# Four buffers for each half of a split weight, the up products' pieces 32 bytes lower, room taken from the dynamic DMAs' scratch

## The chip, the core and the metric

The kernel runs on one core of a Trainium2 chip. The core has a matrix engine (TensorE, PE in the profile, with its weight loads as PEld), a vector engine (DVE), a scalar engine (ACT), GpSimd (POOL) and a queue engine that issues DMAs (SP). All of them work on SBUF, a memory of 128 partitions; an address below is a byte address within a partition. The metric is the device time of one execution in microseconds. Before the change it is 1057.3 us, the median of three runs (1056.95 to 1057.44).

## What is computed

Two decoder layers on 512 tokens of width 1024, in float32: a latent attention mixer and a gated linear attention mixer, each followed by a squared-ReLU MLP with 4096 hidden columns. The part that matters here is the MLP:

```python
def sq_relu_mlp(xn, w_up, w_down):
    hid = jnp.square(jax.nn.relu(xn @ w_up))
    return hid @ w_down

for i in range(DEPTH):              # DEPTH = 2
    xn = rms_norm(x, norm_mix[i])
    x = x + mixer_i(xn)
    x = x + sq_relu_mlp(rms_norm(x, norm_mlp[i]), mlp_w_up[i], mlp_w_down[i])
return rms_norm(x, final_norm)
```

## The kernel before

**Split products.** Every large product is made of three matrix products in float32r: each operand is split into a rounded part (hi) and a rest (lo), and hi x hi, hi x lo and lo x hi are added in PSUM. For weights this is `piece` (L137): it takes a part of a raw weight tile, at most 1,024 float32 per partition, ACT writes the hi part into a tile with the tag `wh` (L104) and DVE the lo part into one with the tag `wl` (L107). Each tag has three buffers of 4,096 bytes, used in turn by all stages, so a fourth piece can be split only when the matmuls of the first have read it.

**The MLP.** `mlp` handles 512 hidden columns at a time, eight blocks in all. The first block and the last have code of their own (`up_first`, and the code behind the loop); the seven between are steps of a Strassen-like scheme (`step`) with seven up products and seven down products in place of eight and eight. An up product (`up_product`, L931, its matmuls in L939) takes four k-tiles of 128, two column halves and three parts: 24 matmuls whose stationary operand is a 128x128 block of the piece (`wh` or `wl`) and whose moving operand is 256 columns of the input. A down product (`down_product`, L941, matmuls in L948) has 12 matmuls whose moving operand is 512 columns of the piece and whose stationary operand is a block of the hidden values. The step's up products come in the order "11", "21", "T2", "T1", "22", "T3", "T4", a down product behind each. For "11", "21" and "22" the moving operand lies in the tiles with the tag `set` that the norm wrote (hi and lo 2,048 bytes apart); for the four with T it lies in tiles `T1` to `T4`, which `quadrants` (L864) fills with sums of input quarters (hi and lo 1,024 bytes apart). A step runs seven times in each of the two MLPs.

**Transfers.** Raw weights come by DMAs that SP issues. Where two weight quarters are added on the way, the second comes by an accumulating DMA that POOL issues (L918, L928): four of them per step. POOL's DMAs keep their descriptors in a scratch at the bottom of SBUF, 16,384 bytes per partition unless the program says otherwise.

**Order.** The kernel is written as one program. The framework puts the instructions of each engine in an order at build time: those that are ready by its own estimate, earliest in the program first; a tile that has no free buffer makes its writer not ready. At run time each engine works strictly in that order and waits on semaphores.

**Addresses.** They follow from the sizes in the code, in the order in which pools and tags are opened, each rounded up to 32 bytes:

| tiles | first byte | remainder by 512 |
|---|---|---|
| scratch of the dynamic DMAs, 16,384 | 0 | 0 |
| constants, and `xT` | 16,384 | |
| `wraw`, 2 of 8,192 | 36,384 | 32 |
| `wh`, 3 of 4,096 | 52,768 | 32 |
| `wl`, 3 of 4,096 | 65,056 | 32 |
| `set`, 16 of 4,096 | 77,344 | 32 |
| `comb` 2 to 5, of 4,096 (in the MLP) | 168,256 | 320 |
| `T2`, `T3`, `T1`, `T4`, 8,192 each (in the MLP) | 184,640 | 320 |
| `comb` 0 and 1 (in the MLP) | 217,408 | 320 |
| `ADh`, `ADl`, 2 of 2,048 each (in the linear attention) | 200,000 | 320 |

A 128x128 block of weights is 512 bytes of a partition, a k-tile of an up product's weights 1,024 bytes and of its input 2,048 or 4,096, so all operands out of one tag share its remainder by 512. That is why the remainder is shown.

Of the kernel before, what the change touches and what calls it, by code (L numbers as in the profile page):

```python
# [10 lines left out]
F32 = mybir.dt.float32  # L11
F32R = mybir.dt.float32r
# [6 lines left out]
P = 128  # L19
# [3 lines left out]
ND = D // P  # L23
# [5 lines left out]
ROPE = 64  # L29
# [6 lines left out]
RANK = 16  # L36
# [14 lines left out]
def trunk_kernel(ctx: ExitStack, tc: tile.TileContext, t_in: dict, out: bass.AP):  # L51
    nc = tc.nc
# [3 lines left out]
    sb = ctx.enter_context(tc.tile_pool(name="sb", bufs=1))  # L56
    count = [0]

    def uname(s):
        count[0] += 1  # L60
        return f"{s}_{count[0]}"
# [14 lines left out]
    def bank(tag):  # L76
        return psum["pool"].tile([P, 512], F32, tag=f"ps_{tag}", bufs=psum["banks"][tag], name=uname("ps"))
# [11 lines left out]
    def tmp(shape=(P, 512), dt=F32):  # L89
        return sb.tile(list(shape), dt, tag="tmp", bufs=6, name=uname("tmp"))  # L90
# [11 lines left out]
    def split(src, hi, lo, hi_eng=ACT, lo_eng=DVE, order=lambda i: i):  # L102
        if hi_eng is ACT:
            order(ACT.activation(hi, src, AF.Copy))  # L104
        else:
            hi_eng.tensor_copy(hi, src)
        lo_eng.tensor_tensor(lo, src, f(hi), ALU.subtract)  # L107
# [26 lines left out]
        SP.dma_start(raw, src)  # L134
        return raw

    def piece(raw, a, n, order=lambda i: i):  # L137
        hi = sb.tile([P, a, n], F32R, tag="wh", bufs=3, name=uname("wh"))
        lo = sb.tile([P, a, n], F32R, tag="wl", bufs=3, name=uname("wl"))
        split(raw, hi, lo, order=order)  # L140
        return hi, lo

    def cut(pair, *idx):
        return tuple(t[idx] for t in pair)
# [56 lines left out]
    def gcol(name, j):  # L201
        c = GAIN_COL[name] + j
        return gains[:, c : c + 1]
# [166 lines left out]
    def col_chunk(w2d, c0, n):  # L370
        return load(w2d[:, c0 : c0 + n].rearrange("(k p) n -> p k n", p=P), w2d.shape[0] // P, n)


    def mla(layer, nrm, first, pools):
# [36 lines left out]
        KH = ND // 2  # L411
        raw = sb.tile([P, ND, 256], F32, tag="wraw", bufs=2, name=uname("wraw"))
        wq = []
        for h in range(2):
            ks = slice(h * KH, (h + 1) * KH)
            SP.dma_start(raw[:, ks], w_in[:, :256].rearrange("(k p) n -> p k n", p=P)[:, ks])
            wq.append(piece(raw[:, ks], KH, 256))
        for j in range(2):
            p = bank("c")
# [10 lines left out]

        raw = col_chunk(w_in, 256, P)
        w = piece(raw, ND, P)
        p = bank("b")
        a_type(p, w, X)
# [2 lines left out]


        raw = col_chunk(w_in, QL + KL, ROPE)
        wr = sb.tile([P, ND, 2, ROPE], F32R, tag="wh", bufs=3, name="w_kr")  # L440
        ACT.activation(wr[:, :, 1, :], raw, AF.Copy)
        DVE.tensor_tensor(wr[:, :, 0, :], raw, f(wr[:, :, 1, :]), ALU.subtract)
        p = bank("b")
# [23 lines left out]
        raw = sb.tile([P, 2, MH, VD], F32, tag="wraw", bufs=2, name="wraw_v")  # L467
        for k in range(2):
            SP.dma_start(raw[:, k], w_ukv[:, k, :, NOPE:])
        wv = [piece(raw[:, k : k + 1].rearrange("p a h c -> p a (h c)"), 1, D) for k in range(2)]  # L470
        V = [[None, None] for _ in range(NT)]
        VP = []
# [13 lines left out]
        for t in range(NT):  # L486
            tk = slice(t * P, (t + 1) * P)
            for hf in range(2):
                p = bank("bc"[hf])
# [15 lines left out]
            if t == 1:  # L505
# [3 lines left out]
                for j in range(2):  # L509
                    y = tmp()  # L510
                    DVE.scalar_tensor_tensor(y, pkv[j], gcol("kvn", 2 * layer + j), r_kv, ALU.mult, ALU.mult)
                    hi, lo = (keep.tile([P, S], F32R, tag=f"ckv{j}{x}", name=f"ckv{j}{x}") for x in "hl")
# [16 lines left out]
        raw = sb.tile([P, 3, MH, ROPE], F32, tag="wraw", bufs=2, name="wraw_qr")  # L529
# [5 lines left out]
        wa = piece(raw3[:, 0:2], 2, 512)  # L535
        wq = [cut(wa, slice(None), 0), cut(wa, slice(None), 1), wb]
        qs = []
        for t in range(NT):
            tk = slice(t * P, (t + 1) * P)
            p = bank("b")  # L540
# [70 lines left out]
        p = bank("c")[:ROPE]  # L611
# [187 lines left out]
    def mlp(layer, nrm, nxt=None):  # L799
# [3 lines left out]
        KH = ND // 2  # L803
        first, second = slice(0, TH), slice(TH, S)
        es = ExitStack()
        fast = es.enter_context(tc.tile_pool(name=f"fast{layer}", bufs=1, reuse_waits="tile"))
# [11 lines left out]
        def comb(i):  # L818
            return fast.tile([P, 2 * S], F32, tag=f"comb{i}", bufs=1, name=uname("comb"))

        def by_k(t, n):
            return t.rearrange("p (k n) -> p k n", k=n)
# [4 lines left out]
        def signed(src, hi, lo, sign):  # L827
            ACT.activation(hi, src, AF.Copy, scale=sign)
            DVE.scalar_tensor_tensor(lo, src, sign, f(hi), ALU.mult, ALU.subtract)
# [34 lines left out]
        def quadrants():  # L864
            lead, trail = range(KH), range(KH, ND)
            quad["11"] = [nrm.parts[k][:, :, first] for k in lead]
            quad["21"] = [nrm.parts[k][:, :, first] for k in trail]
            quad["22"] = [nrm.parts[k][:, :, second] for k in trail]
            t1, t2, t3, t4 = (by_k(comb(i), KH) for i in range(2, 6))
            for k in lead:  # L870
                g1, g2 = (gcol(nrm.g, nrm.g0 + j) for j in (k, k + KH))
                u, v = xT[k], xT[k + KH]
                ACT.activation(t3[:, k], u[:, second], AF.Copy, scale=g1)
                DVE.scalar_tensor_tensor(t3[:, k], v[:, second], g2, t3[:, k], ALU.mult, ALU.subtract)
                DVE.scalar_tensor_tensor(t2[:, k], u[:, first], g1, t3[:, k], ALU.mult, ALU.add)
                DVE.scalar_tensor_tensor(t4[:, k], v[:, first], g2, t2[:, k], ALU.mult, ALU.subtract)
                DVE.scalar_tensor_tensor(t1[:, k], v[:, second], g2, t2[:, k], ALU.mult, ALU.subtract)
            for name, t, sign in (("T2", t2, -1.0), ("T3", t3, 1.0), ("T1", t1, -1.0), ("T4", t4, -1.0)):
                parts = fast.tile([P, KH, 2, TH], F32R, tag=name, name=uname(name))
                signed(t, parts[:, :, 0], parts[:, :, 1], sign)  # L880
                quad[name] = [parts[:, k] for k in lead]
# [47 lines left out]
            return first_part  # L929

        def up_product(t, a, q, start):  # L931
            w = piece(a, KH, 256)
            for j in range(2):
                o = t[:, j * TH : (j + 1) * TH]
                for k in range(KH):
                    wh, wl = cut(w, slice(None), k, slice(j * P, (j + 1) * P))
                    xh, xl = quad[q][k][:, 0], quad[q][k][:, 1]
                    for n, (a_, x_) in enumerate(((wh, xh), (wh, xl), (wl, xh))):
                        PE.matmul(o, a_, x_, start=start and j == 0 and k == 0 and n == 0, stop=k == KH - 1 and n == 2, skip_group_check=True)  # L939
# [11 lines left out]
        def step(b, q, r, after):  # L951
# [24 lines left out]

            z = bank("u")
            up_product(z, a11, "11", True)
            y = bank("u")
            ACT.activation(y, z, AF.Copy)  # L980
# [5 lines left out]
            e = two_banks("e") if opening else begun(d)  # L986

            up_product(y, a12, "21", False)
            finish(y, 0, 0, r)
            DVE.tensor_tensor(a11, s1, a11, ALU.add)  # L990
# [5 lines left out]
            DVE.tensor_tensor(q11, q11, q12, ALU.add)  # L996

            up_product(z, a11, "T2", False)
            u = tmp()
            ACT.activation(u, z, AF.Copy)  # L1000
# [45 lines left out]

        up_first(Q[0])
        quadrants()
        if not nxt:
            residual()  # L1050
# [58 lines left out]
        if nxt:  # L1109
# [6 lines left out]
            for c in range(2):  # L1116
# [10 lines left out]
                for j, p in enumerate(ps_):  # L1127
                    if j % 2 == 0:
                        w = piece(last_raw[c][:, :, j * P : (j + 2) * P], 4, 256)
                    for k in range(4):  # L1130
                        wh, wl = cut(w, slice(None), k, slice(j % 2 * P, (j % 2 + 1) * P))
# [65 lines left out]
    def gla(layer, nrm, vtag, ytag):  # L1197
# [90 lines left out]
        raw = tmp((P, ND, RANK))  # L1288
        ACT.dma_start(raw, w_in[:, 2 * DK + 2 * D :].rearrange("(k p) n -> p k n", p=P))
        R2 = 2 * RANK  # L1290
        wa = sb.tile([P, ND, 3, 2, RANK], F32R, tag="wl", bufs=3, name="wa")
        raw3 = raw.unsqueeze(2).to_broadcast([P, ND, 3, RANK])
        ACT.activation(wa[:, :, :, 1, :], raw3, AF.Copy)
        DVE.tensor_tensor(wa[:, :, :, 0, :], raw3, f(wa[:, :, :, 1, :]), ALU.subtract)
# [6 lines left out]
        p = bank("a")  # L1301
# [352 lines left out]
    for k0, k1 in ((0, 1), (1, 2), (2, 4), (4, 6), (6, 8)):  # L1654
        w = piece(raw0[:, k0:k1], k1 - k0, KL, tc.keep_in_program_order)
# [7 lines left out]
    turns = rope_turns()  # L1663

    O, begun = mla(0, nrm, w0, mla_pools)
    rope_es.close()
    n_mlp0 = Norm(ND, inv_dr, "mlp", 0)
# [19 lines left out]
    mlp(0, n_mlp0, n_mix1)  # L1687
    psum_layout(False)
    Y, begun = gla(0, n_mix1, "B", "B")
    n_mlp1 = Norm(ND, inv_dr, "mlp", ND)  # L1690
    out_proj(t_in["gla_w_o"][0], Y, n_mlp1, begun)
# [52 lines left out]
```

## Time and profile before

| | |
|---|---|
| median of three runs | 1057.3 us |
| the profiled execution's own time | 1057.37 us |
| its span, first to last instruction | 1055.6 us |
| TensorE clock granted, mean | 0.999 |
| instructions | 15,598 |
| HBM traffic | 144.49 MB read, 4.19 MB written |

The profile is of one execution. Busy times are unions of an engine's instructions. Matmuls are pipelined and their ends are modelled, so a matmul's shown length is about twice what it adds to the time; what it adds is read from the distance of starts, or from the chain of waits, which lists the stretches of work that set the end, one behind the other.

### The profile page before, as it was taken

The page shows a single profiled execution, that of the slowest core. Times are in us where ns is not written, and L with a number is a line of the kernel's source. Part 1 is how long each engine was busy: PE and PEld are TensorE (multiplying, and loading weights), DVE is VectorE, ACT ScalarE, POOL GpSimd, SP SyncE. Part 2 cuts the span into 40 slices and gives each one's busy share as a digit, 9 for nine tenths or more (in the row PEclk, how much of TensorE's full clock was granted, in tenths as well). Part 3 has the DMA queues.
Part 4 walks back from the last instruction along what each step waited for, and adds up shares of the span by engine and source line. Part 5 has one row for each costly group of instructions (what it writes and reads, how often), then busy time and mean ns, then how long its engine had stood idle before and what let it go on. Part 6 is the DMA issues. An engine that isn't in the chain of part 4 may idle for free.

```text
span 1055.6 us, 15598 instructions
## 1 busy us (share of the span) xinstructions
PE 1045.5 (99%) x5966; PEld 913.7 (87%) x5966; DVE 876.0 (83%) x1340; ACT 698.6 (66%) x1074; POOL 113.4 (11%) x128
## 2 busy tenths in 40 slices
PE   9999999999999999999999999999999999999997
PEld 7888888889999999998888888878889999999985
DVE  7899977979889889898686498469889989989993
ACT  7667664577777767766445565655667777777784
POOL 7410011201101111000000000000011010010000
PEclk9999999999999999999999999999999999999999
DMA  7311235866966976842322221444496696696622
GB/s 231 90 51 41 81 79 160 238 176 150 235 181 150 229 192 146 221 147 93 90 80 80 80 80 51 126 105 132 110 248 132 178 254 140 176 249 152 165 81 80
DMA packets 120493, 149.97 MB, mean 142 GB/s; under 512 B 9345, under 2 KB 86145, under 8 KB 120289
## 3 DMA queue, kind: packets, MB, share of 16 engines
q1 hardware_dynamic: 95920, 117.76, 34.4%
q0 software_dynamic: 22400, 29.36, 17.4%
q10 hardware_dynamic: 2096, 1.84, 0.6%
q8 instruction: 47, 0.77, 0.3%
q14 instruction: 30, 0.24, 0.1%
HBM read 144.49 MB, written 4.19 MB: 141 GB/s over the span
## 4 chain that ended last, share of the span: by engine, by line
PE 95%; ACT 2%; DVE 2%; issue 0%; DMA 0%; ACTq 0%; SPq 0%; DVEq 0%
PE ps L939 26%; PE ps L948 25%; PE ps L112 10%; PE ps L114 10%; PE ps L113 10%; PE ps L1133 2%; PE ps L1388 2%; PE ps L129 1%; PE ps L1168 1%; PE ps L408 1%; PE ps L1515 1%; DVE wl L107 0%; PE ps L671 0%; PE ps L1438 0%; PE ps L667 0%
## 5 line engine op out<-in xcount | busy, mean ns | idle before, releaser
L948 PE MATMUL ps<-wh,set 128*128 128x512 f32 x784 | 258.5, 390 | 0.0
L107 DVE TENSOR_TENSOR wl<-wraw,wh 128x1024 fp32r<-128x1024 f32 x139 | 169.4, 1221 | 39.7 <-ACT wh L104 39.4
L104 ACT ACTIVATE wh<-wraw 128x1024 fp32r<-128x1024 f32 x139 | 145.9, 1053 | 82.1 <-PE ps L113 38.3
L948 PEld LDWEIGHTS ps<-wh,set 128*128 128x128 f32 x784 | 147.3, 188 | 28.8
L104 ACT ACTIVATE wh<-comb 128x1024 fp32r<-128x1024 f32 x112 | 118.8, 1061 | 62.8 <-PE ps L939 41.9
L939 PE MATMUL ps<-T,wh 128*128 128x256 f32 x896 | 159.8, 279 | 0.0
L948 PE MATMUL ps<-wl,set 128*128 128x512 f32 x392 | 153.7, 392 | 0.0
L107 DVE TENSOR_TENSOR wl<-comb,wh 128x1024 fp32r<-128x1024 f32 x112 | 136.7, 1220 | 18.6 <-ACT wh L104 16.9
L939 PEld LDWEIGHTS ps<-T,wh 128*128 128x128 f32 x896 | 140.5, 188 | 4.5
L939 PE MATMUL ps<-T,wl 128*128 128x256 f32 x448 | 125.1, 279 | 1.0 <-DVE wl L107 1.0
L939 PE MATMUL ps<-set,wh 128*128 128x256 f32 x672 | 122.6, 283 | 0.0
L939 PEld LDWEIGHTS ps<-set,wh 128*128 128x128 f32 x672 | 107.4, 191 | 3.2
L112 PE MATMUL ps<-set,wh 128*128 128x512 f32 x280 | 109.3, 392 | 0.7 <-ACT set L1557 0.3
L113 PE MATMUL ps<-set,wh 128*128 128x512 f32 x280 | 109.4, 391 | 0.0
L114 PE MATMUL ps<-set,wl 128*128 128x512 f32 x280 | 109.0, 390 | 0.0
L939 PE MATMUL ps<-set,wl 128*128 128x256 f32 x336 | 95.2, 283 | 0.0
L939 PEld LDWEIGHTS ps<-T,wl 128*128 128x128 f32 x448 | 84.2, 188 | 1.5 <-DVE wl L107 1.4
L948 PEld LDWEIGHTS ps<-wl,set 128*128 128x128 f32 x392 | 73.8, 188 | 11.6
L928 POOL DMA_DIRECT2D comb<-in_mlp_w_down_dram x28 | 33.6, 1201 | 421.0 <-DMA comb<-in_mlp_w_down_dram 155.5
L939 PEld LDWEIGHTS ps<-set,wl 128*128 128x128 f32 x336 | 64.3, 191 | 0.0
L112 PEld LDWEIGHTS ps<-set,wh 128*128 128x128 f32 x280 | 52.5, 188 | 12.6 <-ACT wh L104 1.0
L114 PEld LDWEIGHTS ps<-set,wl 128*128 128x128 f32 x280 | 52.6, 188 | 11.2 <-DVE wl L107 0.4
(396 smaller groups left out, 2024.2 us busy)
## 6 DMA issues: line engine op xcount, KB each, us to landing
comb<-in_mlp_w_down_dram SPq DMA_DIRECT2D x74, 512.0 KB, 5.0
wraw<-in_mlp_w_up_dram SPq DMA_DIRECT2D x32, 1024.0 KB, 5.8
comb<-in_mlp_w_down_dram POOLq DMA_DIRECT2D x28, 512.0 KB, 7.7
wraw<-in_gla_w_in_dram SPq DMA_DIRECT2D x12, 1024.0 KB, 5.3
comb<-in_mlp_w_up_dram SPq DMA_DIRECT2D x14, 512.0 KB, 3.8
comb<-in_mlp_w_up_dram POOLq DMA_DIRECT2D x14, 512.0 KB, 8.4
wraw<-in_mlp_w_up_dram POOLq DMA_DIRECT2D x14, 512.0 KB, 7.2
wraw<-in_mla_w_o_dram SPq DMA_DIRECT2D x4, 1024.0 KB, 5.0
```

Of the source, the lines that this page charges most:

```text
L104: order(ACT.activation(hi, src, AF.Copy))
L107: lo_eng.tensor_tensor(lo, src, f(hi), ALU.subtract)
L112: PE.matmul(psum, wh, xh, start=start, stop=False)
L113: PE.matmul(psum, wh, xl, start=False, stop=False)
L114: PE.matmul(psum, wl, xh, start=False, stop=stop)
L129: PE.transpose(psum, src, ident[: src.shape[0], : src.shape[0]])
L408: PE.matmul(p, w[:, i, j * P : (j + 1) * P], x, start=start, stop=stop)
L928: POOL.dma_start(t, q(b, *more), accum_op=ALU.add)
L939: PE.matmul(o, a_, x_, start=start and j == 0 and k == 0 and n == 0, stop=k == KH - 1 and n == 2, skip_group_check=True)
L948: PE.matmul(o, x_, w_, start=start and k == 0 and n == 0, stop=k == 1 and n == 2, skip_group_check=True)
L1133: PE.matmul(p, a, x, start=False, stop=k == 3 and n == 2, skip_group_check=True)
L1388: PE.matmul(p[:, t - t0], k[:, t * P : (t + 1) * P], moving[:, t], start=True, stop=True)
```

## The change

Each half of a piece now lives in one of four buffers of 1,152 float32 (4,608 bytes) in place of three of 4,096, and within the buffer it begins at element 128 (byte 512), or, for the pieces of `up_product`, at element 120 (byte 480). Two other users of these tags (`w_kr` and `wa`) take room in the same way. Ahead of the T tiles of the MLP an unused tile of 480 bytes is placed. The scratch of the dynamic DMAs is 4,096 bytes in place of 16,384.

```diff
-    def piece(raw, a, n, order=lambda i: i):
-        hi = sb.tile([P, a, n], F32R, tag="wh", bufs=3, name=uname("wh"))
-        lo = sb.tile([P, a, n], F32R, tag="wl", bufs=3, name=uname("wl"))
+    W_ROOM, W_AT, W_AT_UP = 1152, 128, 120
+
+    def room_for(tag, a, n, at=W_AT):
+        t = sb.tile([P, W_ROOM], F32R, tag=tag, bufs=4, name=uname(tag))
+        return t[:, at : at + a * n].rearrange("p (a n) -> p a n", a=a)
+
+    def piece(raw, a, n, order=lambda i: i, at=W_AT):
+        hi = room_for("wh", a, n, at)
+        lo = room_for("wl", a, n, at)
         split(raw, hi, lo, order=order)
         return hi, lo
...
-        wr = sb.tile([P, ND, 2, ROPE], F32R, tag="wh", bufs=3, name="w_kr")
+        wr = room_for("wh", ND, 2 * ROPE).rearrange("p k (a b) -> p k a b", a=2)
...
+            fast.tile([P, 120], F32, tag="gap", name=uname("gap"))
             for name, t, sign in (("T2", t2, -1.0), ("T3", t3, 1.0), ("T1", t1, -1.0), ("T4", t4, -1.0)):
...
         def up_product(t, a, q, start):
-            w = piece(a, KH, 256)
+            w = piece(a, KH, 256, at=W_AT_UP)
...
-        wa = sb.tile([P, ND, 3, 2, RANK], F32R, tag="wl", bufs=3, name="wa")
+        wa = room_for("wl", ND, 6 * RANK).rearrange("p k (r a b) -> p k r a b", r=3, a=2)
...
-    nc = _bacc.Bacc("TRN2", target_bir_lowering=False, num_devices=1)
+    nc = _bacc.Bacc("TRN2", target_bir_lowering=False, num_devices=1, dynamic_dma_scratch_size=4096)
```

The addresses that follow, by the same reckoning: everything up to `wraw` moves down by 12,288 bytes; `wh` begins at 40,480 and `wl` at 58,912; `set` stays at 77,344, since the two tags grew by 6,144 bytes each. By 512 the remainders are:

| operand | before | after |
|---|---|---|
| pieces of up products | 32 | 0 |
| all other pieces | 32 | 32 |
| `set` tiles | 32 | 32 |
| T tiles, `comb` 0 and 1 | 320 | 288 |

## The prediction

> **What bounds the kernel now.** I read the page first: the span, the busy times, and the chain that ended last.
>
> ```profile
> span 1055.6 us, 15598 instructions
> PE 1045.5 (99%) x5966; PEld 913.7 (87%) x5966; DVE 876.0 (83%) x1340; ACT 698.6 (66%) x1074; POOL 113.4 (11%) x128
> ...
> PE 95%; ACT 2%; DVE 2%; issue 0%; DMA 0%; ACTq 0%; SPq 0%; DVEq 0%
> PE ps L939 26%; PE ps L948 25%; PE ps L112 10%; PE ps L114 10%; PE ps L113 10%; PE ps L1133 2%; PE ps L1388 2%; PE ps L129 1%; PE ps L1168 1%; PE ps L408 1%; PE ps L1515 1%; DVE wl L107 0%; PE ps L671 0%; PE ps L1438 0%; PE ps L667 0%
> ```
>
> The matrix engine is the bound: 95% of the chain, half of it in the MLP's up products (L939) and down products (L948). So only two things can move the time: the pace of the matmuls, or a gap between them. For the pace I read the same chain in order of time over one step of the first MLP; columns are start, length, what.
>
> ```profile
> 290.29 2.87 PE ps L939 x24
> 293.17 2.75 PE ps L948 x12
> 295.91 2.80 PE ps L939 x24
> 298.71 2.75 PE ps L948 x12
> 301.46 2.80 PE ps L939 x24
> 304.26 2.75 PE ps L948 x12
> 307.00 2.87 PE ps L939 x24
> ```
>
> There is no gap: each piece begins where the one before ends. But up products of one and the same shape come in two lengths, 2.87 us and 2.80 us. Which are which, the timeline of PE tells by the operands' names, for two neighbouring up products.
>
> ```profile
> 223.20 0.40 PE L939 MATMUL ps<-T,wh 128*128 128x256 f32 x2
> ...
> 226.00 0.39 PE L948 MATMUL ps<-wh,set 128*128 128x512 f32 x1
> ...
> 228.75 0.40 PE L939 MATMUL ps<-set,wh 128*128 128x256 f32 x2
> ...
> 231.62 0.40 PE L948 MATMUL ps<-wh,set 128*128 128x512 f32 x1
> ```
>
> The one that streams a T tile takes 226.00 - 223.20 = 2.80 us, the one that streams `set` tiles 231.62 - 228.75 = 2.87 us: 117 ns and 120 ns for a matmul. The step above reads 2.87, 2.80, 2.80, 2.87: that is "21", T2, T1, "22" in the program's order. The groups of L939 say the same over all steps.
>
> ```profile
> L939 PE MATMUL ps<-T,wh 128*128 128x256 f32 x896 | 159.8, 279 | 0.0
> L939 PE MATMUL ps<-T,wl 128*128 128x256 f32 x448 | 125.1, 279 | 1.0 <-DVE wl L107 1.0
> L939 PE MATMUL ps<-set,wh 128*128 128x256 f32 x672 | 122.6, 283 | 0.0
> L939 PEld LDWEIGHTS ps<-set,wh 128*128 128x128 f32 x672 | 107.4, 191 | 3.2
> L939 PE MATMUL ps<-set,wl 128*128 128x256 f32 x336 | 95.2, 283 | 0.0
> L939 PEld LDWEIGHTS ps<-T,wl 128*128 128x128 f32 x448 | 84.2, 188 | 1.5 <-DVE wl L107 1.4
> ```
>
> Both the matmul (283 against 279 ns) and the weight load beside it (191 against 188 ns) are some 3 to 4 ns longer with `set`. Nothing waits in either, so something slows the two reads themselves. What differs is where the operands lie: by 512 bytes the moving operand and the weights are 32 and 32 for `set` (difference 0), 320 and 32 for T (difference 288). The next block's weights are loaded while the moving operand streams; with difference 0 the two reads begin at the same place of the 512-byte pattern. That is my reading of the two lengths; no row proves it.
>
> **The change part by part.** *The `set` products.* There are (672 + 336) / 24 = 42. The change moves their weights to remainder 0 and leaves the moving operand at 32: the difference goes from 0 to 32. If any difference but 0 does, they take T's 2.80 us: 42 x 0.07 = **2.9 us less**. No row has the difference 32. The nearest with other differences is the linear attention's `ADh` and `ADl` (moving `set` at 32, weights at 320, difference 224):
>
> ```profile
> 593.08 0.40 PE L1515 MATMUL ps<-set,ADh 128*128 128x256 f32 x2
> ...
> 594.49 0.28 PE L112 MATMUL ps<-set,kth 128*128 128x256 f32 x1
> ```
>
> 12 matmuls in 594.49 - 593.08 = 1.41 us, so 2.82 us for 24. At that pace the gain is 42 x 0.05 = 2.1 us. The far end is the down products' pace: their 12 x 512 columns are as many as an up product's 24 x 256, and take 2.75 us; at that pace 42 x 0.12 = 5.0 us. The near end is no gain. I take 2.9, since T's rows are of the same loop with the same work around it.
>
> *The T products.* (896 + 448) / 24 = 56. Their weights go down by 32 bytes and the unused tile of 480 bytes moves the T tiles from 320 to 288: the difference stays 288. I take **0**. Ends: at 2.82 us they lose 56 x 0.02 = 1.1 us; at `set`'s 2.87 us 56 x 0.07 = 3.9 us; at 2.75 us they gain 56 x 0.05 = 2.8 us.
>
> The Trainium skill speaks against any of this: "TensorE: Matmul & The Clock Gate", Part 2, Step-by-step, says that TensorE reads its moving operand and its weights through two independent ports, so that loading the next weights takes nothing from the matmul that runs. By it the place of the weights is indifferent and the two terms are 0; the two lengths above stand against it, since nothing but the operands' place and their spacing differs, and they leave it open which.
>
> *The fourth buffer.* ACT and POOL wait much, PE hardly:
>
> ```profile
> ACT wh L104 <- PE ps L113: 45.4, 20, 5.0
> ACT wh L104 <- PE ps L939: 41.9, 55, 1.6
> ...
> ACT wh L104 <- PE ps L114: 19.9, 9, 4.4
> ...
> ACT wh L104 <- PE ps L948: 14.4, 24, 0.7
> ```
>
> (who waited, for whom: us in total, times, longest). These 121.6 us are splits held up by full buffers; with a fourth buffer they shorten. But they are ACT's, which is 66% busy. What reaches PE is this:
>
> ```profile
> PEld ps L939 <- DVE wl L107: 1.4, 2, 0.7
> ...
> PEld ps L112 <- ACT wh L104: 1.0, 2, 0.5
> ...
> PEld ps L114 <- DVE wl L107: 0.4, 1, 0.4
> ```
>
> 2.8 us at most. The 1.4 us are the first T product of each MLP, whose weights are a sum that DVE has just made: another buffer doesn't bring that sum forward. Of the other 1.4 us I take **0.3 us less**, as ACT's queue also holds the evacuations there. The other end is a loss: the build orders splits earlier once a buffer is free, and a split of 1.05 us (ACT) or 1.22 us (DVE) that is put ahead of an evacuation delays it. In a step nothing shows for it, since DVE has room:
>
> ```profile
> 290.00:330.00 40.00, 40.00 (x261) 36.52 (x260) 35.85 (x40) 29.23 (x37) 4.97 (x4) 1.00 0.73 185
> ```
>
> (stretch, length, then busy PE, PEld, DVE, ACT, POOL). DVE is busy 35.85 of 40.00 us; a step shorter by 3 x 0.07 us needs the same work in 39.8, which still fits. In the mixers, where PE does wait, I let the 2.8 us double: a loss of up to 2.8.
>
> *Scratch, and tiles moved by 480 bytes.* POOL's DMAs:
>
> ```profile
> q0 software_dynamic: 22400, 29.36, 17.4%
> ...
> comb<-in_mlp_w_down_dram POOLq DMA_DIRECT2D x28, 512.0 KB, 7.7
> ...
> comb<-in_mlp_w_up_dram POOLq DMA_DIRECT2D x14, 512.0 KB, 8.4
> wraw<-in_mlp_w_up_dram POOLq DMA_DIRECT2D x14, 512.0 KB, 7.2
> ```
>
> 56 DMAs of 22400 / 56 = 400 packets. A quarter of the scratch holds fewer of them at once. Should only one fit, each waits for the one before to land: four per step, 2 x 7.7 + 8.4 + 7.2 = 31 us, within the step's 39 (7 x 2.75 + 3 x 2.87 + 4 x 2.80). So **0**; with that cover gone the price is one landing, 8 us, per step. The moved `comb` tiles cost nothing on ACT and DVE: splits from `wraw` (remainder 32) and `comb` (320) take 1053 and 1061 ns on ACT, 1221 and 1220 ns on DVE:
>
> ```profile
> L107 DVE TENSOR_TENSOR wl<-wraw,wh 128x1024 fp32r<-128x1024 f32 x139 | 169.4, 1221 | 39.7 <-ACT wh L104 39.4
> L104 ACT ACTIVATE wh<-wraw 128x1024 fp32r<-128x1024 f32 x139 | 145.9, 1053 | 82.1 <-PE ps L113 38.3
> ...
> L104 ACT ACTIVATE wh<-comb 128x1024 fp32r<-128x1024 f32 x112 | 118.8, 1061 | 62.8 <-PE ps L939 41.9
> L107 DVE TENSOR_TENSOR wl<-comb,wh 128x1024 fp32r<-128x1024 f32 x112 | 136.7, 1220 | 18.6 <-ACT wh L104 16.9
> ```
>
> **The sum**: -2.9 + 0 - 0.3 + 0 = -3.2 us. The span goes from 1055.6 to 1052.4; with the 1.8 us around it (1057.37 - 1055.6) that is 1054.2, and 1054.1 against the median of 1057.3, from which the profiled execution is 0.07 away.
>
> **The rivals.** *The place of the weights is not the cause.* The lengths may come from the spacing of hi and lo (2,048 bytes in `set`, 1,024 in T) or from the part of memory. Then the up products stay as they are and the time is 1057.3 - 0.3 = 1057.0. For it: T and `set` differ in these too. Against it: `ADh` streams `set` tiles at 2.82 us, not 2.87. The skill's two ports would give the same time.
>
> *The start of the moving operand decides (the other side).* T's 320 is a multiple of 64, the `set` tiles' 32 is not, and after the change T's 288 is not either. Then `set` products stay at 2.87 us and the T products join them, 56 x 0.07 = 3.9 us more: 1057.3 + 3.9 - 0.3 = 1060.9. It decides if T products read over 2.82 us with moving operands at 288. For it: it sorts the two lengths as well as the difference does. Against it: `ADh` again, whose moving operand lies at 32.
>
> *Both kinds get faster.* The weights' start at a multiple of 512 helps by itself, and all up products go to the down products' 2.75 us: 5.0 + 2.8 + 0.3 = 8.1 us less, 1049.2. For it: 0.05 us is there to be had. Against it: `ADh` weights begin at a multiple of 64 and do not reach it.
>
> *The new order costs more than the pace gives.* Splits ahead of evacuations in the mixers and output products, 2.8 us, with the `set` products only at 2.82: 1057.3 + 2.8 - 2.1 = 1058.0; with as much again in the steps, 1060.8.
>
> **How the numbers follow.** Forecast 0.58 (its own range 1053.0 to 1055.2: 2.1 to 3.4 us from the pace, the rows being rounded to 0.01 us, and 0 to 0.9 from the buffer), not the cause 0.13, start of the moving operand 0.10, both faster 0.10, order 0.09. A measurement of this kernel can tell about 0.2%, 2.1 us, from no change. Faster: 0.56 of the forecast's 0.58, and 0.10, and some 0.02 of the rest, 0.68. Slower: 0.10 and 0.06 of the order's 0.09, 0.16. Within: 0.16. The range goes from the faster rival, 1049.0, to just past the slower ones, 1061.0.
>
> **What would show it.** In the chain of a step every up product of `set` and of T reads 2.80 us; matmuls of L939 with `set` read 279 and their weight loads 188 ns; L948 stays at 2.75. ACT's waits for PE fall well below 121.6 us, and PE's 2.8 us hardly. The prediction is wrong if `set` stays at 2.87 us, if T rises, or if PE waits for `wh` or `wl` where it did not.

## The result, and the profile after

The changed kernel takes 1054.36 us (median of 9 runs, 1053.9 to 1055.96) against 1057.3 us (9 runs, 1056.88 to 1057.53). The ratio is 0.9973, with a 95% interval of 0.9965 to 0.9982: faster by 0.27%. Predicted were 1054.1 us. The profiled execution took 1054.16 us with a span of 1052.4.

The first fence is the head of the page after and its chain of waits; L939 and L948 of before are L946 and L955 now.

```profile
span 1052.4 us, 15648 instructions
PE 1043.0 (99%) x5966; PEld 910.3 (86%) x5966; DVE 874.2 (83%) x1340; ACT 702.6 (67%) x1074; POOL 113.8 (11%) x128
...
PE 93%; DVE 3%; ACT 2%; DMA 1%; issue 1%; ACTq 0%; SPq 0%; DVEq 0%
```

PE is still the bound. The chain of a step, in order of time (start, length, what):

```profile
290.35 2.80 PE ps L946 x24
293.15 2.75 PE ps L955 x12
295.90 2.80 PE ps L946 x24
...
307.01 2.80 PE ps L946 x24
```

The up products with `set` read 2.80 us, those with T stay there. Three pairs take 307.01 - 290.35 = 16.66 us, against 307.00 - 290.29 = 16.71 before. That is 0.05 us less, where one `set` product alone should give 0.07: something else has become a little longer. The groups of the up products and of the splits:

```profile
L104 ACT ACTIVATE wh<-wraw 128x1024 fp32r<-128x1024 f32 x139 | 147.0, 1061 | 115.2 <-PE ps L946 40.0
...
L946 PE MATMUL ps<-T,wl 128*128 128x256 f32 x448 | 124.9, 279 | 0.0
L946 PE MATMUL ps<-set,wh 128*128 128x256 f32 x672 | 119.7, 280 | 0.0
...
L946 PEld LDWEIGHTS ps<-set,wh 128*128 128x128 f32 x672 | 105.2, 188 | 3.5
```

With `set`, matmul and weight load have come down from 283 and 191 to 280 and 188 ns, where 279 and 188 were expected. The 1.0 us that T's matmuls waited for DVE's `wl` is gone, which was not predicted. ACT's splits wait more than before: 115.2 us against 82.1 in this group.

Where the time went, stage by stage, is read from the starts of the same matmul in both kernels. First before, then after, in the timeline of PE (start, length, what):

```profile
205.61 0.40 PE L939 MATMUL ps<-set,wh 128*128 128x256 f32 x2
...
474.20 0.40 PE L939 MATMUL ps<-T,wh 128*128 128x256 f32 x2
...
750.75 0.48 PE L939 MATMUL ps<-set,wh 128*128 128x256 f32 x2
...
770.39 0.40 PE L939 MATMUL ps<-T,wh 128*128 128x256 f32 x2
...
1021.38 0.40 PE L939 MATMUL ps<-T,wh 128*128 128x256 f32 x2
```

```profile
206.61 0.40 PE L946 MATMUL ps<-set,wh 128*128 128x256 f32 x2
...
223.55 0.40 PE L946 MATMUL ps<-T,wh 128*128 128x256 f32 x2
...
473.45 0.40 PE L946 MATMUL ps<-T,wh 128*128 128x256 f32 x2
...
749.17 0.48 PE L946 MATMUL ps<-set,wh 128*128 128x256 f32 x2
...
768.24 0.40 PE L946 MATMUL ps<-T,wh 128*128 128x256 f32 x2
...
1018.13 0.40 PE L946 MATMUL ps<-T,wh 128*128 128x256 f32 x2
```

The rows are: the first up product of an MLP ("11" of the first step), "T1" of the same step (223.20 before, in the prediction), "T4" of the seventh step. The differences, with three kernels of the experiments below beside them, in us against before (taken from the traces to the nanosecond, so that the rounded rows can be 0.01 off; the sums are those of the spans):

| stretch | after | three buffers, up pieces lower | four buffers, all pieces at 32 | T pieces at 32, one of four held in the first mixer |
|---|---|---|---|---|
| up to the first up product (first mixer) | +1.00 | +0.07 | +1.12 | -0.22 |
| first up product to "T1" of the first step | -0.65 | -0.07 | -0.58 | -0.65 |
| "T1" of the first step to "T4" of the seventh | -1.09 | -1.09 | 0.00 | -1.27 |
| to the first up product of the second MLP (second mixer) | -0.83 | -0.06 | -0.83 | -0.83 |
| to its "T1" | -0.58 | -0.03 | -0.55 | -0.61 |
| to its "T4" | -1.09 | -1.09 | 0.00 | -1.27 |
| rest | +0.04 | +0.01 | 0.00 | +0.05 |
| sum | -3.20 | -2.27 | -0.84 | -4.79 |

The kernels with three buffers and with all pieces at 32 have one part of the change each; together they give -3.11 of the change's -3.20, so the two parts hardly touch each other.

### The profile page after: what moved, and what is told of

It reads as the page before. It is cut to its first block, busy times and chain, and to the rows that moved or that the text cites. A ratio compares the mean times of both kernels' runs of the same rounds, so it can differ in the third digit from the quotient of the medians.

```text
span 1052.4 us, 15648 instructions
## 1 busy us (share of the span) xinstructions
PE 1043.0 (99%) x5966; PEld 910.3 (86%) x5966; DVE 874.2 (83%) x1340; ACT 702.6 (67%) x1074; POOL 113.8 (11%) x128
## 4 chain that ended last, share of the span: by engine, by line
PE 93%; DVE 3%; ACT 2%; DMA 1%; issue 1%; ACTq 0%; SPq 0%; DVEq 0%
PE ps L955 26%; PE ps L946 26%; PE ps L112 10%; PE ps L114 10%; PE ps L113 10%; PE ps L1140 2%; PE ps L1395 1%; PE ps L129 1%; PE ps L1175 1%; PE ps L414 1%; PE ps L1522 1%; DVE wl L107 1%; DVE acc L245 0%; PE ps L1445 0%; PE ps L677 0%
## 5 line engine op out<-in xcount | busy, mean ns | idle before, releaser
L955 PE MATMUL ps<-wh,set 128*128 128x512 f32 x784 | 259.2, 392 | 0.1
L104 ACT ACTIVATE wh<-wraw 128x1024 fp32r<-128x1024 f32 x139 | 147.0, 1061 | 115.2 <-PE ps L946 40.0
L955 PEld LDWEIGHTS ps<-wh,set 128*128 128x128 f32 x784 | 147.1, 188 | 29.3 <-ACT set L104 0.5
L946 PE MATMUL ps<-T,wh 128*128 128x256 f32 x896 | 159.8, 279 | 0.0
L955 PE MATMUL ps<-wl,set 128*128 128x512 f32 x392 | 153.7, 392 | 0.0
L946 PEld LDWEIGHTS ps<-T,wh 128*128 128x128 f32 x896 | 140.4, 188 | 4.7
L946 PE MATMUL ps<-T,wl 128*128 128x256 f32 x448 | 124.9, 279 | 0.0
L946 PE MATMUL ps<-set,wh 128*128 128x256 f32 x672 | 119.7, 280 | 0.0
L112 PE MATMUL ps<-set,wh 128*128 128x512 f32 x280 | 109.2, 391 | 0.5 <-ACT set L1564 0.3
L114 PE MATMUL ps<-set,wl 128*128 128x512 f32 x280 | 109.2, 390 | 0.0
L946 PEld LDWEIGHTS ps<-set,wh 128*128 128x128 f32 x672 | 105.2, 188 | 3.5
L946 PE MATMUL ps<-set,wl 128*128 128x256 f32 x336 | 93.8, 279 | 0.0
L946 PEld LDWEIGHTS ps<-T,wl 128*128 128x128 f32 x448 | 84.2, 188 | 0.1
L955 PEld LDWEIGHTS ps<-wl,set 128*128 128x128 f32 x392 | 73.6, 188 | 11.7
L946 PEld LDWEIGHTS ps<-set,wl 128*128 128x128 f32 x336 | 63.2, 188 | 0.0
L112 PEld LDWEIGHTS ps<-set,wh 128*128 128x128 f32 x280 | 52.5, 188 | 11.6 <-issue 0.6
L114 PEld LDWEIGHTS ps<-set,wl 128*128 128x128 f32 x280 | 52.6, 188 | 10.8
```

What stands on the lines that cost most here:

```text
L112: PE.matmul(psum, wh, xh, start=start, stop=False)
L114: PE.matmul(psum, wl, xh, start=False, stop=stop)
L955: PE.matmul(o, x_, w_, start=start and k == 0 and n == 0, stop=k == 1 and n == 2, skip_group_check=True)
```

## The experiments

**The pace without the fourth buffer.** The change with three buffers. The scratch is 12,288 bytes, with which every remainder by 512 is that of the change.

```diff
-        t = sb.tile([P, W_ROOM], F32R, tag=tag, bufs=4, name=uname(tag))
+        t = sb.tile([P, W_ROOM], F32R, tag=tag, bufs=3, name=uname(tag))
...
-    nc = _bacc.Bacc("TRN2", target_bir_lowering=False, num_devices=1, dynamic_dma_scratch_size=4096)
+    nc = _bacc.Bacc("TRN2", target_bir_lowering=False, num_devices=1, dynamic_dma_scratch_size=12288)
```

> Three buffers as before (of 4,608 bytes, pieces at 512, up products' at 480), the unused tile ahead of T, scratch 12,288 so that it fits: the places of the change without the fourth buffer. If the places set the pace of the up products and the fourth buffer only changes the order of ACT and DVE: up products 2.80 us, down products a little over 2.75 as in the changed kernel, stalls of the T2 products and of the output products as before, about 2.2 us less than before (1055.1). If the pace came with the fourth buffer: 2.87 us and 1057.3.

Measured: 1055.09 us (11 runs), ratio 0.9979 (0.997 to 0.9987). All up products take 2.798 us (medians of the distances of starts), down products 2.755. The wait of the first T products stays, as PE's waits (who, for whom: us, times, longest) show:

```profile
PE ps L946 <- DVE wl L107: 1.2, 2, 0.6
```

So the pace comes from the place of the weights, with the order of before: 2.2 us by the medians (1057.26 for the kernel before, measured beside it), 2.27 in the table.

**Four buffers without the place.** The change with the up products' pieces at byte 512 like all others, and without the unused tile.

```diff
-            fast.tile([P, 120], F32, tag="gap", name=uname("gap"))
...
-            w = piece(a, KH, 256, at=W_AT_UP)
+            w = piece(a, KH, 256)
```

> Four buffers, all pieces at 512, no unused tile: the fourth buffer without the new places. If the places set the pace: up products of set 2.87 us and of T 2.80, down products 2.75, the T2 stall of 0.7 us in each MLP gone, the first mixer about 1 us longer, the output product of the second mixer about 1 us shorter; 0.8 to 1.2 us less than before (1056.3). If the fourth buffer brought the whole gain: 1054.4.

Measured: 1056.44 us (11 runs), ratio 0.9991 (0.9982 to 0.9999). Its chain shows the paces of before:

```profile
290.84 2.87 PE ps L945 x24
...
296.46 2.80 PE ps L945 x24
```

The buffers alone gain 0.8 us, which the interval just sets apart from no change, and the table shows that this is a loss of 1.1 us in the first mixer against gains of 0.58, 0.83 and 0.55.

**The scratch alone.** The kernel before with 4,096 bytes of scratch.

```diff
-    nc = _bacc.Bacc("TRN2", target_bir_lowering=False, num_devices=1)
+    nc = _bacc.Bacc("TRN2", target_bir_lowering=False, num_devices=1, dynamic_dma_scratch_size=4096)
```

> The kernel before with a scratch of 4,096 bytes for the dynamic DMAs and nothing else. If a smaller scratch costs nothing: 1057.3, and POOL's DMAs land in 7 to 8.5 us as before. If it makes them wait for room: landing well over 8.5 us, and more than 1057.3 if a product waits for a weight.

Measured: 1057.19 us (10 runs), ratio 1.0 (0.999 to 1.0009). Nothing, as predicted: POOL's three kinds of DMA landed in 7.9, 8.6 and 7.3 us (medians), against 7.7, 8.4 and 7.2.

**Which difference counts.** Two kernels, the change with another start for the weights of each up product of a step (in float32 elements; element 128 is remainder 32 by 512).

```diff
+    AT = {'11': 112, '21': 96, 'T2': 128, 'T1': 112, '22': 64, 'T3': 56, 'T4': 64}
...
+    AT = {'11': 8, '21': 124, 'T2': 80, 'T1': 116, '22': 104, 'T3': 100, 'T4': 88}
...
-            w = piece(a, KH, 256, at=W_AT_UP)
+            w = piece(a, KH, 256, at=AT[q])
```

> The changed kernel with another place for each of the seven up products; differences of the moving operand's and the weights' remainders by 512: product 11 64, 21 128, 22 256 (set tiles), T2 256, T1 320, T3 32, T4 0. If a difference of 0 is what is slow: T4 alone 2.87 us, all others 2.80. If the weights' start on a multiple of 64 bytes is what is fast: only T3 has it, 11, 21 and 22 at 2.87 us. If both operands count by themselves, T4 stays at 2.80.

> The changed kernel with seven more differences, by 256 bytes, which is the period that the first such run showed (256 reads as 0): product 11 224, 21 16, 22 96 (set tiles), T2 192, T1 48, T3 112, T4 160. If only the distance between the two places counts, 224 reads as 32 does, 2.80 us, and 192 as 64, 2.82; if it counts which of the two is ahead, they are slower. No place is expected under 2.80 us by either.

The up products in the chain of the first of the two, in the order "11", "21", T2, T1, "22", T3, T4:

```profile
285.50 2.82 PE ps L947 x24
...
291.06 2.89 PE ps L947 x24
...
296.70 2.87 PE ps L947 x24
...
302.32 2.82 PE ps L947 x24
...
307.88 2.87 PE ps L947 x24
...
313.51 2.80 PE ps L947 x24
...
319.05 2.87 PE ps L947 x24
```

Medians over the undisturbed steps of both kernels, 12 to 14 for each product and alike within 0.001 us, by the difference between the moving operand and the weights, taken by 256 bytes:

| difference | 0 | 16 | 32 | 48 | 64 | 96 | 112 | 128 | 160 | 192 | 224 |
|---|---|---|---|---|---|---|---|---|---|---|---|
| us | 2.872 | 2.813 | 2.798 | 2.800 | 2.824 | 2.870 | 2.864 | 2.889 | 2.818 | 2.827 | 2.838 |

None of the three theories noted before the first kernel fits: differences of 128 and 256 by 512 are slow too. T2, "22" and T4 stood at 256, 256 and 0 by 512 and all took 2.872 to 2.873: the pattern repeats after 256 bytes, and T is slowed like `set`. By 256 the difference 288 of the T products is 32. So the change gave the `set` products just the difference that T had. Of the two theories noted before the second kernel, the one by which 224 reads like 32, the same distance on the other side, falls.

In these two kernels the moving operand always begins at 32 by 256 (32 or 288 by 512), so by themselves they cannot tell the difference from the weights' own place. Other kernels can. With weights at 32, as `set` had them, T at 320 took 2.802 us before the change, and with both at 64, in the kernel with every operand on 64 bytes below, `set` took 2.872 us: what the differences 32 and 0 took here. The two kernels took 1058.08 us each in a single run, since most of the places are worse than 32.

**Down products' neighbour.** In the kernel after, the matmul between a down product and the next up product has another step:

```profile
223.31 0.40 PE L955 MATMUL ps<-wh,set 128*128 128x512 f32 x1
223.55 0.40 PE L946 MATMUL ps<-T,wh 128*128 128x256 f32 x2
```

0.24 us from start to start. Before, the same matmul starts 0.22 us ahead of the T product at 223.20:

```profile
222.98 0.39 PE L948 MATMUL ps<-wh,set 128*128 128x512 f32 x1
```

The medians are 235 and 227 ns, once for each of the 98 down products: 0.8 us. While it runs, the weights that are loaded next are the up product's, at remainder 0; a down product ahead of weights at 32 keeps 227 ns. This can be undone for the T products: without the unused tile they lie at 320, and with weights at 32 their difference is still 32 by 256.

```diff
-            fast.tile([P, 120], F32, tag="gap", name=uname("gap"))
...
-            w = piece(a, KH, 256, at=W_AT_UP)
+            w = piece(a, KH, 256, at=W_AT if q[0] == "T" else W_AT_UP)
```

> The changed kernel, but only the up products of set at byte 480; those of T at 512 as before, and no unused tile: T keeps its 2.80 us. If the 8 ns more of the last matmul of a down product come from the next up product's first weights lying at another place than the down product's piece, the 56 down products ahead of T lose them: 0.4 us less than the changed kernel (1054.0). If they come from something else in the change: as the changed kernel, 1054.4.

Measured: 1053.57 us (5 runs), ratio 0.9967 (0.9954 to 0.9979). T products take 2.802 us, and the down products ahead of them are back at 2.744 to 2.747 us; the stretch of the steps gains 1.27 us instead of 1.09. The interval overlaps that of the change, so that the gain over it rests on the trace.

**The loss in the first mixer.** The same kernel, with one of the four buffers of each tag held until the first mixer has ended (`wh` and `wl` then lie ahead of `wraw`, with the same remainders).

```diff
+    held = [room_for(tag, 1, 8) for tag in ("wh", "wl")]
+    for t in held:
+        POOL.memset(f(t), 0.0)
...
+    for t in held:
+        POOL.tensor_copy(f(t)[:, 0], f(O[MH - 1][1])[:, :8])
```

> As the run before, and one buffer of each tag is held through the first mixer (four tiny GpSimd instructions more), so that three are left there. If the first mixer's 1 us comes from the order that four buffers give there, it goes: 1053.0, with the first mixer as long as before the change. If it comes from the places or from the smaller scratch, it stays: 1054.0.

Measured: 1052.53 us (5 runs), ratio 0.9957 (0.9943 to 0.9971). The first up product begins 0.22 us before that of the kernel before, instead of 1.00 us behind it. In the kernel after the weight loads' waits show what the loss was made of:

```profile
PEld ps L129 <- DVE pr L704: 1.0, 4, 0.3
PEld ps L112 <- DVE set L489: 0.7, 2, 0.5
```

Both are products of the first mixer that wait for a DVE result; the waits for a third, `PTl`, grew from 0.3 to 0.6 us. With the buffers held the first is back at the 0.5 us of before, `PTl` at 0.3, and the one for L489 is gone:

```profile
PEld ps L129 <- DVE pr L708: 0.5, 2, 0.3
```

For L489 (L483 before) DVE's order shows the reason. First after, then before:

```profile
45.05 1.23 DVE L107 TENSOR_TENSOR wl<-wraw_kn,wh 128x1024 fp32r<-128x1024 f32 x1 [0.41 <-ACT wh L104]
46.20 2.72 DVE L489 SCALAR_TENSOR_TENSOR set<-ps,cols,set 128x512 fp32r<-128x512 f32 x4
```

```profile
44.47 0.17 DVE L497 COPY cols<-ps 128x12 f32<-128x12 f32 x1 [0.83 <-PE ps L129]
45.40 3.39 DVE L483 SCALAR_TENSOR_TENSOR set<-ps,cols,set 128x512 fp32r<-128x512 f32 x5 [0.76 <-ACT set L482]
```

The copy starts at 44.47 us in both. After it, the kernel after has a split of 1.23 us first, and what PE waits for begins 0.80 us later. One of the four waits for `pr` is of the same kind (a split at 124.75 us directly ahead of the `pr` at 125.87); the two at 143.33 and 144.73 us, 0.16 and 0.30 us long, have no split directly ahead, and what makes them late stays open. That the loss comes with the use of the fourth buffer in this stage is shown.

**The unused tile.** The change without it: T tiles at 320 instead of 288, all other places as in the change.

```diff
-            fast.tile([P, 120], F32, tag="gap", name=uname("gap"))
```

> The changed kernel without the unused tile: T tiles stay at 320, their weights at 0, difference 64. If the difference alone counts: T 2.82 us, 56 x 0.026 = 1.5 us more, less what the down products behind gain (0.015 each, 0.8). If the start of the moving operand on a multiple of 64 is worth something of its own, T is at or under 2.80.

Measured: 1052.14 us (one run), 2.2 us less than the change, where the difference alone would have made it some 0.7 us more. The chain, "21" to T1:

```profile
290.29 2.80 PE ps L945 x24
293.09 2.75 PE ps L954 x12
295.84 2.73 PE ps L945 x24
298.57 2.79 PE ps L954 x12
301.36 2.72 PE ps L945 x24
```

T products took 2.723 us, 113 ns for a matmul, though their difference is 64 by 256, for which the sweep had 2.824. The down products behind them rose to 2.790. Two operands that both begin on a multiple of 64 bytes was one explanation.

**Every operand on 64 bytes.** The kernel before with 32 unused bytes in two places; then the change with the same, and several differences.

```diff
+    const.tile([P, 8], F32, name="pad_a")
...
+    sb.tile([P, 8], F32, tag="pad_b", name="pad_b")
```

```diff
+    AT = {"11": 128, "21": 112, "T2": 112, "T1": 128, "22": 96, "T3": 80, "T4": 96}
+    AT_DOWN = [128, 16, 32, 48, 128, 16, 128]
...
-            fast.tile([P, 120], F32, tag="gap", name=uname("gap"))
+            fast.tile([P, 112], F32, tag="gap", name=uname("gap"))
...
-            w = piece(a, KH, 256, at=W_AT_UP)
+            w = piece(a, KH, 256, at=AT[q])
...
-            wh, wl = piece(a, 2, 512)
+            wh, wl = piece(a, 2, 512, at=AT_DOWN[downs[0] % 7])
```

> The kernel before, with 32 unused bytes at the end of the constants and 32 more behind the last tile of its first pool, so that every operand of a matmul begins on a multiple of 64 bytes (before, wraw, wh, wl, set at remainder 32 by 64). All differences between the moving operand and the weights stay as they were; three buffers, the order of before. Theory A (the difference alone counts): set up products stay at 2.87 us, T up products 2.80 to 2.82, down products 2.75: 1057 to 1058. Theory B (an operand that begins off a multiple of 64 costs each matmul some 3 ns beside what the difference does): T up products go to the 2.72 us of the kernel without the unused tile, set up products to 2.79 or 2.80, and if 512-wide products gain as much per matmul, down products to some 2.67: 1046 to 1053.

> The kernel after, with every operand of a matmul on a multiple of 64 bytes and the difference between the moving operand and the weights (by 256 bytes) varied over the products of a step: up products 11: 0, 21: 64, 22: 128, T2: 64, T1: 0, T3: 192, T4: 128; the pieces of the seven down products in turn against the blocks they meet: 0, 64, 128, 192, 0, 64, 0. Theory A (the difference alone counts, 0 slow): 11 and T1 2.87 us, T2 and 21 2.82, the others 2.80. Theory B (a start off 64 costs each matmul some 3 ns): all others 2.72 as in the kernel without the unused tile, 11 and T1 2.79 or 2.80; down products whose pieces stand at another difference are at or below 2.75.

Measured: 1059.03 us (11 runs), ratio 1.0017 (1.0008 to 1.0026), slower by 0.2%; the other kernel 1060.34 us (one run). "21" and T2 of the first kernel:

```profile
290.02 2.87 PE ps L940 x24
...
295.64 2.83 PE ps L940 x24
```

T2 of the second, at the very remainders (320 and 0) that gave 2.72 without the unused tile:

```profile
296.63 2.83 PE ps L950 x24
```

In the first kernel the differences did not all stay as they were; the text before the run was wrong in this. Both unused tiles lie ahead of the T tiles, which so moved by 64 bytes, to 384 by 512, while the weights moved by 32: T's difference became 320, 64 by 256. The kernel is slower by what this costs: its T products take 2.830 us for 2.802 (56 x 0.028 = 1.6 us) and the down products behind them 2.757 for 2.744 (0.7 us); its first up product begins 0.53 us earlier than before, which stays unexplained.

So starts on multiples of 64 do not give the 2.72 us, and the starts of the two operands do not fix the pace by themselves. The second kernel has more that the difference alone does not explain: "22" and T4, both at 128, took 2.877 and 2.844 us, against 2.889 in the sweep. So the sweep's medians hold beside the down products of that sweep, whose pieces began at 32. The down products in the second kernel, with their pieces at other differences, took up to 2.807 us.

**What ran ahead.** The kernel without the unused tile, with another place for the pieces of some down products (64 ahead of T2, 0 ahead of T3, 480 ahead of "11"), and T1 and T4 moved by 512 and 1,024 bytes.

```diff
+    AT_DOWN = [128, 8, 128, 128, 120, 128, 112]
...
+                if name in ("T1", "T4"):
+                    fast.tile([P, 128], F32, tag="gap" + name, name=uname("gap"))
...
-            wh, wl = piece(a, 2, 512)
+            wh, wl = piece(a, 2, 512, at=AT_DOWN[downs[0] % 7])
```

> The kernel without the unused tile, where T up products took 2.72 us at starts 320 and 0 by 512, against 2.82 in the kernel with every operand on 64 bytes, at the same starts. Two things are varied over the T products of a step, to find what sets these apart: the piece of the down product ahead (32 as before; ahead of T2 64, ahead of T3 0; ahead of 11 480), and the T tile's address (T1 512 bytes higher, T4 1,024 higher, their starts by 512 unchanged). Theory E (the pace is inherited: two reads that start in step stay in step, so what ran ahead decides): T2 and T3, or one of them, go to 2.82, T1 and T4 stay at 2.72. Theory M (a longer period of the address, 1,024 bytes): T1 goes to 2.82, T4, T2 and T3 stay. Theory N (neither; something else in the other kernel): all four stay at 2.72. The set up products stay at 2.80 in all, 11 perhaps not under E. Time: 1052 if all stay, 0.7 us more for each T product that goes up.

Measured: 1055.09 us (one run). T2, T1, T3, T4 in the chain:

```profile
295.73 2.82 PE ps L949 x24
...
301.31 2.73 PE ps L949 x24
...
312.43 2.83 PE ps L949 x24
...
318.02 2.72 PE ps L949 x24
```

Those behind an unchanged down product keep 2.72 us though they were moved; those behind a changed one lose 0.1 us though neither of their own operands was moved. Theory E fits, theories M and N fall: at the starts 320 and 0 an up product has two paces, and the one it runs at follows from where the down product ahead of it read. That down product is not all that counts: in the sweep "11" and T1 had the difference 64 too, behind pieces at 32 like T1 and T4 here, and took 2.824 us with their weights at 480.

**The best version.** The kernel without the unused tile, with the held buffers of above.

> The kernel without the unused tile (all pieces of down products at 32, the T tiles at 320 and up pieces at 0 by 512, T up products at 2.72 us), and one buffer of each tag held until the first mixer has ended, as in the other kernel with held buffers. If both gains are independent: 1052.1 less about 1.2 us for the first mixer, 1050.9, ratio to before 0.994; the first mixer 0.3 us shorter than before instead of 1 us longer, T up products 2.72 us, the down products behind them 2.79. If the pace of T products hangs on the order of the splits too: T at 2.80 to 2.82 and 1053 to 1055.

Measured: 1051.02 us (5 runs, 1050.63 to 1051.67), ratio 0.9941 (0.9928 to 0.9955). T products stay at 2.723 us, and the first up product starts 0.16 us before that of the kernel before. The two gains add up: the held buffers are worth 1.1 us here (1052.14 to 1051.02) and 1.0 with the T pieces at 32 (1053.57 to 1052.53).

## Why the prediction was right, and where its terms were not

*The `set` products: right, with the reason half right.* They went to T's 2.80 us, 42 x (2.872 - 2.798) = 3.1 us, and it is the place of the weights that did it (three buffers, 2.27 us in all). That the difference decides was guessed from two rows. For the places that the change has, the sweep bears it out, with a period of 256 instead of 512; at the differences 64 and 128 the later kernels show that it is not the whole rule. `ADh`'s 2.82 us, the other row that was weighed, was no near neighbour: its difference of 224 took 2.838 in the sweep. Of the rivals, "the place is not the cause" falls by the three-buffer kernel, "the start of the moving operand decides" by T at 288 with 2.80 us, and "both kinds get faster" by the same chain.

The Trainium skill's page "TensorE: Matmul & The Clock Gate" (Part 2, Step-by-step), by which the moving operand and the weights are read through two ports of their own, would have had this term at nothing. The 2.872 and 2.798 us of the same products, with nothing but the place of the weights between them, say otherwise here.

*The T products: right.* 2.802 to 2.798 us.

*A term that was missing: the boundary.* The prediction left the down products at 2.75 us, and at two decimals they are. At three they rose from 2.746 to 2.755, since the last matmul of each now runs beside the loading of weights at another place. That is 98 x 0.009 = 0.9 us, which made the pace worth 2.3 us instead of 2.9.

*The fourth buffer: right in sign, wrong in size and in its working.* Taken were 0.3 us less; by the table it gave 0.8 alone and 0.9 on top of the places. The step that failed reads "The 1.4 us are the first T product of each MLP, whose weights are a sum that DVE has just made: another buffer doesn't bring that sum forward". The trace of before has the sum, its split by ACT and by DVE, and the wait:

```profile
199.21 1.23 DVE L990 TENSOR_TENSOR wraw<-comb,wraw 128x1024 f32<-128x1024 f32 x1
...
213.73 1.23 DVE L107 TENSOR_TENSOR wl<-wraw,wh 128x1024 fp32r<-128x1024 f32 x1 [0.49 <-ACT wh L104]
```

```profile
212.65 1.05 ACT L104 ACTIVATE wh<-wraw 128x1024 fp32r<-128x1024 f32 x1
```

```profile
215.01 0.39 PE L939 MATMUL ps<-T,wl 128*128 128x256 f32 x1 [0.51 <-DVE wl L107]
```

The sum was ready at 199.21 + 1.23 = 200.44, 12 us before its split began. PE waited for the split, and that stood late in ACT's order. After, ACT and DVE make the same split so early that nothing waits:

```profile
209.49 1.06 ACT L104 ACTIVATE wh<-wraw 128x1024 fp32r<-128x1024 f32 x1 [1.23 <-PE ps L946]
```

```profile
211.15 1.22 DVE L107 TENSOR_TENSOR wl<-wraw,wh 128x1024 fp32r<-128x1024 f32 x1
```

DVE is done at 212.37, and T2 starts at 214.97. The two other waits that the prediction named, for `wh` at L112 and `wl` at L114, are gone too; they lay in the product behind the second mixer and gave most of its 0.83 us. Against this stands the loss of 1.0 us in the first mixer, the rival "the new order costs more than the pace gives": its mechanism, a split ahead of a result that PE needs, is seen there in some of the waits, in one stage of three, and it was too small to decide.

*ACT's waits for PE did not fall.* They were expected well below 121.6 us. The four kinds quoted there are 126.9 after. This fits splits that run ahead until the fourth buffer is full, as they ran ahead until the third was; no run shows it by itself.

*Scratch: right*, 1057.19 us with it alone. What it would cost in a step that has no time to hide a landing, no run shows.

*The total* was met to 0.3 us because the missing 0.9 us at the boundary and the 0.6 us too little for the buffer nearly cancel. That closeness was luck.

## What to carry to other kernels

When matmuls of one shape come in two lengths and nothing waits, compare the byte addresses of the moving operand and of the weights, and vary one of them over the products of a single kernel before choosing; count also the last matmul ahead of each place where they change. Another buffer mostly acts through the order in which the build puts the splits, so it can gain in one stage and lose in the next: look up when a late operand could have been made, not only which engine made it late.

## What the hardware showed that was not expected

A matmul of 256 columns in float32r took 113, 117 or 120 ns by where its moving operand and the weights lie, with a pattern that repeats after 256 bytes (2.798 us for 24 at a difference of 32, 2.872 at 0, 2.889 at 128). With the moving operand at 320 and the weights at 0 by 512 the same product took 2.72 or 2.82 us, by where the down product ahead of it had read, and kept that pace over its 24 matmuls. A clash of the two reads would explain this, but no run shows the mechanism.
